# Feed-forward networks that begin by tiles of tokens, and GpSimd without elementwise work at stage boundaries

## The chip, the cores and the metric

The kernel runs on one core of one Trainium2 chip. The metric is the device time of one execution in microseconds (us). The engines are TensorE (PE; its weight loads are listed as PEld), VectorE (DVE), ScalarE (ACT), GpSimd (POOL), and SyncE (SP), whose queue issues the transfers.

## What is computed

256 tokens of 1024 columns pass two blocks. The first has two layers (attention, mixture of experts, an embedding gate). The second, which the change is mostly about, is:

```python
n = modulate(rmsnorm(h, g_ffn1[l]), sh1, sc1)
h = h + 0.5 * gt1 * swiglu(n, w1_gate[l], w1_up[l], w1_down[l])
n = modulate(rmsnorm(h, g_mix[l]), sh2, sc2)
h = h + gt2 * hybrid_mixer(n, w_in[l], w_pool[l], pool_scale[l], w_out[l])
n = modulate(rmsnorm(h, g_ffn2[l]), sh3, sc3)
h = h + 0.5 * gt3 * swiglu(n, w2_gate[l], w2_up[l], w2_down[l])
return rmsnorm(h, g_final)
```

`swiglu(n, wg, wu, wd)` is `(silu(n @ wg) * (n @ wu)) @ wd` with 2816 hidden columns, and `modulate(n, shift, scale)` is `n * (1 + scale) + shift`. The shifts, scales and gates are nine vectors from `silu(c) @ w_ada + b_ada`.

## The kernel before

All of h [128 partitions, 2 tiles of tokens, 1024] stays in SBUF. Products are in three passes over fp32r parts: an operand is split into a high part `hi` and what it leaves, `lo`, and `mm3` (L302 to 306) issues hi·hi, hi·lo and lo·hi. Weights come in units of 1 MB (`unit`, nine buffers `raw`) and are split in halves of a unit by `halves` (L278): ACT writes `hi` (L291), and DVE writes `lo` as raw minus hi (L292). There are four buffers of each, so four halves at most. While the counter `self.aside` is not zero, `lo` is made by POOL instead of DVE: for the first four halves behind each modulation, and for one piece at the start of each embedding gate.

`modulated_T` begins each of the three stages of the second block (FFN 1, mixer, FFN 2). It computes 1/rms of both tiles of tokens (`rstd`: two ACT squares with a sum per tile, L334, then a chain of nine DVE operations on one column, L314 to L337), fills PE with the columns of w_ada that are planned there (`fill`, `ada`, L1447), transposes h on PE, lays 1/rms along the rows (`rbc`), and then makes for each of the 8 blocks of columns f = h·gain·rbc (DVE), hi = f + shift (ACT), lo = f + shift − hi (DVE). For the mixer it does this by tiles of tokens (`head`, L403 to 411); for the two FFNs over all 256 tokens at once (L419 to 427).

An FFN goes over groups of 4 (last 2) blocks of 128 hidden columns. `dense_T` has the weight stationary and the 256 tokens moving, so gate and up come out transposed; a tanh on ACT and two DVE operations make the hidden values, which are split again (`hT`) and go into `down` one group later. `dense` has the tokens stationary and 512 weight columns moving; with `tail` (or `head`) its last (or first) chunk takes all of the first tile of tokens, then all of the second, and keeps all four split halves until the second pass. `add_gated` adds the last product of a stage to h (L1482, L1483), `finish` norms the rows and writes them out.

The order of the instructions on each engine is made by the framework's scheduler from the program order, the readiness by its own model, and a priority: `ahead_by(name)` moves instructions that many places ahead (`K["hp"]`: rstd 30, silu 200, split 60). Each engine then executes its queue in that order.

Of the kernel before, what the change touches and what calls it, by code (L numbers as in the profile page):

```python
# [8 lines left out]
F32 = mybir.dt.float32  # L9
F32R = mybir.dt.float32r  # L10
# [6 lines left out]
P = 128  # L17
# [41 lines left out]
class Packed:  # L59
    """Columns of a [128, n] array by name."""  # L60
# [55 lines left out]
def moving_units(w, widths, step=4):  # L116
    """Blocks of 128 rows by `step`, one after the other, a column chunk at a time."""
# [79 lines left out]
class Block:  # L197
    def __init__(self, ctx, tc, A, out, c_at, m_at, s_at, dbg=None):
# [14 lines left out]
        self.flip = 0  # L213
        self.waiting = []
# [3 lines left out]
    # -- small helpers -------------------------------------------------  # L218
# [59 lines left out]
    def halves(self, raw, n, k):  # L278
        """The unit's two parts, in halves of k/2 blocks of rows: f32r high parts and what they leave."""
# [28 lines left out]
    def rsqrt(self, y, v, n):  # L308
        """y = 1/sqrt(v/n) for positive v and n = 4**j: Newton's steps from the exponent's guess."""
# [14 lines left out]

    def rstd(self, tiles=(0, 1)):
        """1/rms of each token's row of h, a column for each of the tiles of tokens."""
        nc = self.nc
        n = len(tiles)
        with self.ahead_by("rstd"):
            ss = self.stat([P, n, 2], "ss")  # L330
            for half in range(2):
                for i, t in enumerate(tiles):
                    junk = self.wk.tile([P, 512], BF16, tag="xn", name="junk", bufs=4)
                    nc.scalar.activation(junk, self.h[:, t, half * 512:(half + 1) * 512], AF.Square,  # L334
                                         accum_out=ss[:, i, half:half + 1])
# [15 lines left out]
    def gained_T(self, gains, head):  # L351
        """h by each of the gains, transposed and in two parts; 1/rms is left to the products' rows."""
# [34 lines left out]
    def modulated_T(self, gain, shift, fill, head=False):  # L387
        """The normed rows by gain plus shift, transposed and in two parts."""
        nc = self.nc
        r = [self.rstd([t]) for t in range(2)]  # L390
        self.fill(*fill)
        self.aside = K["aside"]
        self.fine = bool(K["fmod"])
        with self.ahead_by("mod"):
            hi, lo = self.e([P, KT, T], F32R), self.e([P, KT, T], F32R)
            if head:
                for t in range(2):
                    sl = slice(t * P, (t + 1) * P)
                    ps = [self.psb([P, 4, P]) for _ in range(2)]
# [12 lines left out]
                return hi, lo  # L412
            ps = [self.psb([P, 2, T]) for _ in range(KT // 2)]
            pr = self.psa([P, T])
            rb = self.wk.tile([P, T], F32, tag="xn", name="rbc", bufs=4)
            for t in range(2):
                sl = slice(t * P, (t + 1) * P)
                for kk in range(KT):
                    nc.tensor.transpose(ps[kk // 2][:, kk % 2, sl], self.h[:, t, kk * P:(kk + 1) * P], self.ident)  # L419
                nc.tensor.transpose(pr[:, sl], r[t].to_broadcast([P, P]), self.ident)  # L420
                nc.vector.tensor_copy(rb[:, sl], pr[:, sl])
            for kk in range(KT):
                f = self.wk.tile([P, T], F32, tag="xn", name="xn", bufs=4)
                g, b = gain[:, kk:kk + 1], shift[:, kk:kk + 1]
                nc.vector.scalar_tensor_tensor(f, ps[kk // 2][:, kk % 2], g, rb, op0=OP.mult, op1=OP.mult)
# [1241 lines left out]
```

## Time and profile before

| | us |
|---|---|
| times of three runs | 1141.69, 1140.62, 1138.66 |
| median | 1140.62 |
| span of the profiled execution | 1135.9 |
| median less that span | 4.7 |
| PE busy, DVE busy, ACT busy, POOL busy | 1070.6, 701.9, 516.2, 74.3 |

The span goes from the first to the last instruction of the profiled execution; which of the times is that execution's is not listed, so the 4.7 us is taken from the median. A busy PE here means that matmuls are in flight: a matmul's listed duration is longer than the distance to the next one's start, so products are costed by the distance of starts.

### The profile page before, as it was taken

What the parts mean: (1) busy time and instruction counts of PE and PEld (TensorE: products, weight loads), DVE (VectorE), ACT (ScalarE), POOL (GpSimd) and SP (SyncE); (2) the same over time, 40 slices, a digit from 0 to 9 for tenths busy, and PEclk for the clock granted to TensorE, in tenths of its full rate; (3) what the DMA queues carried; (4) which work ended last, traced back from release to release, by engine and by line L of the source; (5) the groups of instructions that cost most, each with busy time, mean ns of one, the idle gap of its engine ahead of it and who ended that gap; (6) DMA issues with size and microseconds to landing.
All of it is one profiled execution on the core that took longest, in us unless ns stands there. A gap on an engine that the chain in (4) does not pass through costs nothing.

```text
span 1135.9 us, 18442 instructions
## 1 busy us (share of the span) xinstructions
PE 1070.6 (94%) x7133; PEld 833.2 (73%) x7133; DVE 701.9 (62%) x1672; ACT 516.2 (45%) x995; POOL 74.3 (7%) x61
## 2 busy tenths in 40 slices
PE   7999999999989999998987999999989979999995
PEld 6885548666457667665545999899879759999994
DVE  6786784644378966543467656565684775554555
ACT  5446584222267674221254444433544634444443
POOL 3000000210010002100003000000210030000001
PEclk9999999899999999999999999999989989999998
DMA  9746767599975485798886456745675344554401
GB/s 375 296 185 262 277 225 304 196 372 396 416 273 170 180 336 198 286 389 323 314 350 242 168 186 213 284 173 186 224 301 175 123 185 149 174 187 159 146 22 38
DMA packets 46508, 268.57 MB, mean 236 GB/s; under 512 B 5328, under 2 KB 7120, under 8 KB 20432
## 3 DMA queue, kind: packets, MB, share of 16 engines
q1 hardware_dynamic: 46416, 267.34, 62.9%
q8 instruction: 58, 0.95, 0.3%
q14 instruction: 34, 0.28, 0.1%
HBM read 266.27 MB, written 1.05 MB: 235 GB/s over the span
## 4 chain that ended last, share of the span: by engine, by line
PE 46%; DVE 5%; ACT 1%; issue 0%; ACTq 0%; DVEq 0%
PE b L305 8%; PE b L304 8%; PE b L306 8%; PE a L304 5%; PE a L306 5%; PE a L305 5%; PE a L1054 1%; DVE nq L319 1%; DVE h L1483 1%; PE a L1094 1%; DVE rstd L323 1%; PE a L1107 1%; PE b L1460 1%; DVE w L1482 1%; PE b L1033 0%
## 5 line engine op out<-in xcount | busy, mean ns | idle before, releaser
L292 DVE TENSOR_TENSOR lo<-raw,hi 128x1024 fp32r<-128x1024 f32 (+2 forms) x220 | 256.1, 1167 | 197.7 <-ACT hi L291 195.5
L291 ACT ACTIVATE hi<-raw 128x1024 fp32r<-128x1024 f32 (+2 forms) x234 | 234.3, 1008 | 262.3 <-PE b L305 144.6
L304 PE MATMUL b<-e,hi 128*128 128x256 f32 x768 | 219.7, 286 | 2.9 <-ACT e L426 2.9
L305 PE MATMUL b<-e,hi 128*128 128x256 f32 x768 | 219.3, 285 | 0.1
L306 PE MATMUL b<-e,lo 128*128 128x256 f32 x768 | 218.9, 285 | 0.0
L304 PE MATMUL a<-hi,e 128*128 128x512 f32 (+2 forms) x512 | 199.9, 391 | 2.4 <-ACT e L364 1.8
L305 PE MATMUL a<-lo,e 128*128 128x512 f32 (+2 forms) x512 | 198.0, 387 | 0.0
L306 PE MATMUL a<-hi,e 128*128 128x512 f32 (+2 forms) x512 | 197.2, 387 | 0.5 <-DVE e L365 0.5
L304 PEld LDWEIGHTS b<-e,hi 128*128 128x128 f32 x768 | 149.2, 194 | 4.7 <-ACT e L426 3.6
L305 PEld LDWEIGHTS b<-e,hi 128*128 128x128 f32 x768 | 149.1, 194 | 1.0 <-DVE e L427 0.7
L306 PEld LDWEIGHTS b<-e,lo 128*128 128x128 f32 x768 | 149.1, 194 | 0.0
L304 PEld LDWEIGHTS a<-hi,e 128*128 128x128 f32 x512 | 96.8, 189 | 23.1 <-ACT e L364 2.9
L306 PEld LDWEIGHTS a<-hi,e 128*128 128x128 f32 x512 | 96.1, 188 | 20.7 <-DVE e L365 2.1
L305 PEld LDWEIGHTS a<-lo,e 128*128 128x128 f32 x512 | 96.9, 189 | 18.9 <-DVE lo L292 0.9
L1054 PE MATMUL a<-raw,e 128*32 128x256 f32 x832 | 73.5, 383 | 1.1 <-DVEq L1291 0.8
L579 ACT ACTIVATE p<-p,m 128x128 f32<-128x128 f32 (+1 forms) x96 | 42.6, 447 | 8.9 <-DVE m L574 6.6
L484 DVE TENSOR_TENSOR h<-h,a 128x512 f32<-128x512 f32 x48 | 32.0, 684 | 22.0 <-PE a L1107 14.7
L1054 PEld LDWEIGHTS a<-raw,e 128*32 128x32 f32 x832 | 31.4, 109 | 18.8 <-issue 2.1
L292 POOL TENSOR_TENSOR lo<-raw,hi 128x1024 fp32r<-128x1024 f32 (+1 forms) x14 | 31.4, 2267 | 205.1 <-ACT hi L291 205.0
L1097 ACT ACTIVATE w<-a,sv 128x512 fp32r<-128x512 f32 x32 | 21.6, 687 | 48.0 <-PE a L1094 47.6
L1094 PE MATMUL a<-wd,hT 128*32 128x512 f32 x256 | 43.3, 607 | 0.0
L1107 PE MATMUL a<-w,GT 128*128 128x512 f32 x128 | 36.3, 416 | 6.2 <-ACT w L1097 5.1
(322 smaller groups left out, 1424.3 us busy)
## 6 DMA issues: line engine op xcount, KB each, us to landing
raw<-in_ffn SPq DMA_DIRECT2D x62, 1024.0 KB, 4.8
raw<-in_moe_gu SPq DMA_DIRECT2D x52, 1024.0 KB, 8.4
raw<-in_w_ada SPq DMA_DIRECT2D x36, 1024.0 KB, 5.0
wd<-in_moe_dn SPq DMA_DIRECT2D x64, 512.0 KB, 7.0
raw<-in_w_gate SPq DMA_DIRECT2D x8, 1024.0 KB, 11.1
raw<-in_w_m_in SPq DMA_DIRECT2D x8, 1024.0 KB, 5.5
raw<-in_w_a_in SPq DMA_DIRECT2D x7, 1024.0 KB, 11.1
e<-in_moe_gu SPq DMA_DIRECT2D x6, 1024.0 KB, 9.5
```

The source lines that it names most:

```text
L291: nc.scalar.activation(hi[:, sl], raw[:, at], AF.Copy)
L292: eng.tensor_tensor(lo[:, sl], raw[:, at], hi[:, sl], op=OP.subtract)
L304: mm(out, l[0], r[0], start=start, stop=False, **kw)
L305: mm(out, l[0], r[1], start=False, stop=False, **kw)
L306: mm(out, l[1], r[0], start=False, stop=stop, **kw)
L319: nc.vector.scalar_tensor_tensor(q, y, h, y, op0=OP.mult, op1=OP.mult)
L484: self.nc.vector.tensor_tensor(self.h[:, t, sl], self.h[:, t, sl], ps, op=OP.add)
L579: nc.scalar.activation(p, p, AF.Exp, bias=m[:, i:i + 1], scale=-1.0, accum_out=den[:, i:i + 1])
L1054: nc.tensor.matmul(pgs[pp][32 * x:32 * x + 32], xg[:, k, o:o + 32], wg[kk][:, x], start=(k == 0), stop=(k == KT - 1))
L1094: nc.tensor.matmul(py[32 * x:32 * x + 32], hT[:, 32 * x:32 * x + 32], wd[2 * n + x // 2][:, x % 2], start=True, stop=True)
L1097: nc.scalar.activation(yh[:, sl], py, AF.Identity, scale=cw)
L1107: nc.tensor.matmul(ps, GT[:, t * P:(t + 1) * P], y[:, n * 512:(n + 1) * 512], start=(b == 0), stop=(b == len(back) - 1))
```

## The change

- `self.aside` goes: every `lo` of a weight is made by DVE.
- `modulated_T` always goes by tiles of tokens: 1/rms, transposes and modulation of the first tile, then 1/rms of the second, the fill with w_ada columns, and the second tile.
- The sums of squares are issued where the last addition to h is made (`square_new`, in the second embedding gate and in `add_gated`), a half row at a time, and `rstd` takes them from there.
- The first group of each FFN uses `dense` with `head` for gate and up (tokens stationary), the hidden values are made in rows, and PE transposes them; the other groups stay.
- The PSUM banks of `down` (`acc`) are taken only after the first group. The w_ada products of the fills at stage starts use the pool `pa`, and their copies to SBUF come after the modulation (`later`).
- `finish` multiplies by 1/rms and by the gain in one DVE operation; before, POOL multiplied by the gain, and ACT and DVE by 1/rms.
- Docstrings and comments go (no instruction depends on them).

```diff
-                eng = nc.vector if self.aside == 0 or j < pieces - 1 else nc.gpsimd
...
+    def square(self, out, t, half):
+        junk = self.wk.tile([P, 512], BF16, tag="xn", name="junk", bufs=4)
+        self.nc.scalar.activation(junk, self.h[:, t, half * 512:(half + 1) * 512], AF.Square, accum_out=out)
+
+    def square_new(self, ci, t):
+        if ci + t == 0:
+            self.squares = self.stat([P, 2, 2], "squares", bufs=1)
+        with self.ahead_by("rstd"):
+            self.square(self.squares[:, t, ci:ci + 1], t, ci)
...
-    def modulated_T(self, gain, shift, fill, head=False):
-        r = [self.rstd([t]) for t in range(2)]
-        self.fill(*fill)
-        self.aside = K["aside"]
+    def modulated_T(self, gain, shift, fill, head=True):
+        hi, lo = self.e([P, KT, T], F32R), self.e([P, KT, T], F32R)
+        r = [None, None]
         with self.ahead_by("mod"):
             if head:
                 for t in range(2):
                     sl = slice(t * P, (t + 1) * P)
+                    r[t] = self.rstd([t])
+                    if t:
+                        self.squares = None
+                        self.fill(*fill)
...
+        for rows, ps in self.copies:
+            self.copy(rows, ps)
...
             self.nc.vector.tensor_tensor(self.h[:, t, sl], self.h[:, t, sl], y, op=OP.add)
+            self.square_new(ci, t)
...
-        acc = [[self.psa([P, 512]) for _ in range(2)] for _ in range(2)]
...
+            if gi == 0:
+                def put_up(ci, t, ps):
+                    with self.ahead_by("silu"):
+                        f = self.w4([P, 512])
+                        nc.scalar.activation(f, gates[t], AF.Tanh, scale=0.5)
+                        nc.vector.scalar_tensor_tensor(f, f, 1.0, gates[t], op0=OP.add, op1=OP.mult)
+                        nc.vector.scalar_tensor_tensor(f, f, 0.5, ps, op0=OP.mult, op1=OP.mult)
+                        rows.append(f)
+
+                off = self.dense(x, name, [512], lambda ci, t, ps: gates.append(ps), off, head=True)
+                off = self.dense(x, name, [512], put_up, off, head=True)
+                nb = 0
+                for b in range(2):
+                    with self.ahead_by("silu"):
+                        ps = self.psb([P, 2, T])
+                        for j in range(2):
+                            for t in range(2):
+                                nc.tensor.transpose(ps[:, j, t * P:(t + 1) * P],
+                                                    rows[t][:, (2 * b + j) * P:(2 * b + j + 1) * P], self.ident)
+                        self.parts(hT[0][:, 2 * b:2 * b + 2], hT[1][:, 2 * b:2 * b + 2], ps)
+            else:
+                for _ in range(2):
+                    off = self.dense_T(x, name, n, lambda b, ps: banks.append(ps), off)
...
-                nc.gpsimd.tensor_tensor(o[:, t, sl], self.h[:, t, sl], self.g_final[:, sl], op=OP.mult)
-            for half in range(2):
-                sl = slice(half * 512, half * 512 + 512)
-                self.copy(o[:, t, sl], o[:, t, sl], r)
+                nc.vector.scalar_tensor_tensor(o[:, t, sl], self.h[:, t, sl], r, self.g_final[:, sl], op0=OP.mult,
+                                               op1=OP.mult)
```

## Rows read from the trace of the kernel before

**Rows 1.** The page's busy time by engine (share of the span, count of instructions), and the granted clock of TensorE in 40 slices of the span, in tenths of full speed.

```profile
PE 1070.6 (94%) x7133; PEld 833.2 (73%) x7133; DVE 701.9 (62%) x1672; ACT 516.2 (45%) x995; POOL 74.3 (7%) x61
...
PEclk9999999899999999999999999999989989999998
```

**Rows 2.** Busy time of each engine in six stretches: from the last matmul of the stage before to the end of the first product of FFN 1, of the mixer and of FFN 2, each followed by the part of it in which the clock was low. Columns: stretch, its length, busy us and count of PE, PEld, DVE, ACT, POOL, granted clock, share of the DMA engines, GB/s.

```profile
609.80:638.40 28.60, 20.70 (x147) 17.01 (x147) 21.34 (x34) 12.87 (x20) 9.58 (x4) 0.82 0.64 246
619.70:629.90 10.20, 6.34 (x26) 5.76 (x27) 8.13 (x20) 2.75 (x7) 1.58 (x1) 0.50 0.88 371
821.00:844.10 23.10, 19.72 (x99) 13.91 (x99) 20.83 (x59) 12.71 (x29) 5.14 (x2) 0.85 0.79 314
827.90:834.70 6.80, 5.56 (x17) 4.33 (x18) 6.46 (x28) 2.04 (x7) 0.00 (x0) 0.50 1.01 426
920.00:947.10 27.10, 19.13 (x131) 16.21 (x131) 20.87 (x41) 9.78 (x17) 6.76 (x3) 0.81 0.47 180
926.90:937.10 10.20, 6.25 (x25) 5.16 (x26) 7.95 (x27) 3.82 (x9) 0.00 (x0) 0.50 0.67 281
```

**Rows 3.** Timeline of PE at the start of FFN 1: start, duration, engine, line, operation, operands, count of merged instructions, and in brackets the idle time before and what ended it.

```profile
611.62 1.90 PE L1447 MATMUL b<-raw,c 128*32 128x512 f32 x16
613.45 1.23 PE L419 MATMUL b<-consts,h 128*128 128x128 f32 x8
...
622.06 0.48 PE L420 MATMUL a<-consts,rstd 128*128 128x128 f32 x1 [6.41 <-DVE rstd L323]
623.98 0.58 PE L304 MATMUL b<-e,hi 128*128 128x256 f32 x1 [1.44 <-ACT e L426]
```

**Rows 4.** Timeline of DVE at the start of FFN 1: the first and last of the chain of tile 0, then a copy from PSUM, and from 613.21 the chain of tile 1.

```profile
607.47 0.16 DVE L337 SCALAR_TENSOR_TENSOR ssv<-ss 128x1 f32<-128x1 f32 x1 [0.79 <-ACT junk L334]
...
609.07 0.16 DVE L323 SCALAR_TENSOR_TENSOR rstd<-nq,rstd 128x1 f32<-128x1 f32 x1
...
612.04 0.69 DVE L267 COPY w<-b 128x512 f32<-128x512 f32 x1
613.21 1.17 DVE L337 SCALAR_TENSOR_TENSOR ssv<-ss 128x1 f32<-128x1 f32 x1 [0.48 <-ACT junk L334]
...
616.73 2.26 DVE L323 SCALAR_TENSOR_TENSOR rstd<-nq,rstd 128x1 f32<-128x1 f32 x1
...
622.90 1.27 DVE L425 SCALAR_TENSOR_TENSOR xn<-b,mods,rbc 128x256 f32<-128x256 f32 x3
...
625.27 1.26 DVE L425 SCALAR_TENSOR_TENSOR xn<-b,mods,rbc 128x256 f32<-128x256 f32 x3
```

**Rows 5.** Timeline of POOL at the same place.

```profile
611.69 9.58 POOL L292 TENSOR_TENSOR lo<-raw,hi 128x1024 fp32r<-128x1024 f32 x4 [23.60 <-ACT hi L291]
```

**Rows 6.** Timeline of DVE at the start of FFN 2.

```profile
917.93 1.92 DVE L337 SCALAR_TENSOR_TENSOR ssv<-ss 128x1 f32<-128x1 f32 x1 [1.70 <-ACT junk L334]
...
927.34 0.68 DVE L1482 TENSOR_TENSOR w<-a,w 128x512 f32<-128x512 f32 x1
```

**Rows 7.** Timeline of DVE at the start of the mixer; the last three are the modulation by tiles of tokens, three blocks of columns to a row.

```profile
822.55 2.68 DVE L1483 TENSOR_TENSOR h<-h,w 128x512 f32<-128x512 f32 x1
825.15 2.30 DVE L319 SCALAR_TENSOR_TENSOR nq<-rstd,nh 128x1 f32<-128x1 f32 x1
...
830.91 0.87 DVE L409 SCALAR_TENSOR_TENSOR xn<-b,mods,rbc 128x128 f32<-128x128 f32 x3
831.73 0.94 DVE L411 SCALAR_TENSOR_TENSOR e<-xn,mods,e 128x128 fp32r<-128x128 f32 x3
832.58 0.86 DVE L409 SCALAR_TENSOR_TENSOR xn<-b,mods,rbc 128x128 f32<-128x128 f32 x3
```

**Rows 8.** Timeline of PE around the mixer's first two products: the ends of a product with 512 columns moving, sixteen small matmuls between, and a product with 256 columns moving.

```profile
843.69 0.39 PE L305 MATMUL a<-lo,e 128*128 128x512 f32 x1
843.92 0.39 PE L306 MATMUL a<-hi,e 128*128 128x512 f32 x1
844.14 1.84 PE L1460 MATMUL b<-consts,w 128*128 128x1 f32 x16
845.85 0.37 PE L304 MATMUL b<-e,hi 128*128 128x256 f32 x1
...
846.53 0.28 PE L306 MATMUL b<-e,lo 128*128 128x256 f32 x1
846.65 0.28 PE L304 MATMUL b<-e,hi 128*128 128x256 f32 x1
```

**Rows 9.** Groups of instructions by line and shape in the stretch 600 to 835 us: busy us, mean ns of one, idle time before.

```profile
L292 DVE TENSOR_TENSOR lo<-raw,hi 128x1024 fp32r<-128x1024 f32 x59 | 72.2, 1224 | 63.3 <-ACT hi L291 61.4 <-DMA raw<-in_ffn 1.8
L291 ACT ACTIVATE hi<-raw 128x1024 fp32r<-128x1024 f32 x67 | 70.7, 1058 | 93.8 <-PE b L305 63.8 <-PE a L306 20.5 <-issue 7.9
...
L1524 DVE SCALAR_TENSOR_TENSOR w<-w,b 128x512 f32<-128x512 f32 x11 | 7.5, 681 | 0.0
...
L1523 ACT ACTIVATE w<-b 128x512 f32<-128x512 f32 x11 | 6.5, 589 | 2.4 <-PE b L306 2.4
```

**Rows 10.** Timeline of DVE at the end of the program.

```profile
1122.35 1.40 DVE L1483 TENSOR_TENSOR h<-h,w 128x512 f32<-128x512 f32 x1
...
1126.37 1.18 DVE L1483 TENSOR_TENSOR h<-h,w 128x512 f32<-128x512 f32 x1
...
1131.72 0.49 DVE L263 TENSOR_SCALAR e<-e,rstd 128x512 f32<-128x512 f32 x1
```

More of the change, by code (lines that the diff above doesn't have):

```diff
@@ L213, in __init__ @@
         self.flip = 0
+        self.squares = None
+        self.copies = []
         self.waiting = []
@@ L329, in rstd @@
         with self.ahead_by("rstd"):
-            ss = self.stat([P, n, 2], "ss")
-            for half in range(2):
[L332 to L335, printed above, removed]
+            if self.squares is not None:
+                ss = self.squares[:, tiles[0]:tiles[0] + n]
+            else:
+                ss = self.stat([P, n, 2], "ss")
+                for half in range(2):
+                    for i, t in enumerate(tiles):
+                        self.square(ss[:, i, half:half + 1], t, half)
             v = self.stat([P, n], "ssv")
@@ L411, in modulated_T @@
                         nc.vector.scalar_tensor_tensor(lo[:, kk, sl], f, b, hi[:, kk, sl], op0=OP.add, op1=OP.subtract)
[L412 to L425, printed above, removed]
-                nc.scalar.activation(hi[:, kk], f, AF.Identity, bias=b)
-                nc.vector.scalar_tensor_tensor(lo[:, kk], f, b, hi[:, kk], op0=OP.add, op1=OP.subtract)
+        for rows, ps in self.copies:
+            self.copy(rows, ps)
+        self.copies = []
         return hi, lo
@@ L1424, in ada_start, with ada @@
         self.mods = self.cp.tile([P, 9, KT], F32, name="mods")
-    def ada(self, n, psum):
+    def ada(self, n, psum, later=False):
         nc = self.nc
@@ L1449, in ada @@
         rows = self.w4([P, 512])
-        self.copy(rows, ps)
+        if later:
+            self.copies.append((rows, ps))
+        else:
+            self.copy(rows, ps)
         self.waiting.append((n, rows))
@@ L1483, in put @@
             self.nc.vector.tensor_tensor(self.h[:, t, sl], self.h[:, t, sl], y, op=OP.add)
+            self.square_new(ci, t)
         return put
@@ L1513, in ffn @@
             hT = (both[:, 0], both[:, 1])
-            banks = []
-            for _ in range(2):
-                off = self.dense_T(x, name, n, lambda b, ps: banks.append(ps), off)
+            banks, gates, rows = [], [], []
+            nb = n // 2
+            if gi == 0:
[17 more added lines that the diff above has]
+                        self.parts(hT[0][:, 2 * b:2 * b + 2], hT[1][:, 2 * b:2 * b + 2], ps)
+            else:
+                for _ in range(2):
+                    off = self.dense_T(x, name, n, lambda b, ps: banks.append(ps), off)
             self.ada_put()
-            nb = n // 2
             for b in range(nb):
@@ L1527, in ffn @@
             if pending:
+                if acc is None:
+                    acc = [[self.psa([P, 512]) for _ in range(2)] for _ in range(2)]
                 down(*pending)
@@ L1597, in finish @@
                 sl = slice(half * 512, half * 512 + 512)
-                nc.gpsimd.tensor_tensor(o[:, t, sl], self.h[:, t, sl], self.g_final[:, sl], op=OP.mult)
-            for half in range(2):
-                sl = slice(half * 512, half * 512 + 512)
-                self.copy(o[:, t, sl], o[:, t, sl], r)
+                nc.vector.scalar_tensor_tensor(o[:, t, sl], self.h[:, t, sl], r, self.g_final[:, sl], op0=OP.mult,
+                                               op1=OP.mult)
                 nc.sync.dma_start(self.out[t * P:(t + 1) * P, sl], o[:, t, sl])
@@ L1606, in fill @@
         for n in K["fill"].get(f"{where}:{j}", ()):
-            self.ada(n, self.psb if where.startswith("ffn") else self.psa)
+            self.ada(n, self.psb if where == "ffn0" else self.psa,
+                     where in ("ffn", "mixer"))
         if where in ("nsa", "moba"):
```

7 lines of the change are left out of this document (3 added, 4 removed).

## The prediction

> **What bounds the kernel now.** Read the page's busy times first [rows 1]: TensorE is busy 94% of the span, DVE 62%, GpSimd 7%. A share of 94% leaves little to win by feeding TensorE better in general, so the next view is where it does not run at full rate: the granted clock by slices shows single eights, and the windows show what lies there. At the start of FFN 1, mixer and FFN 2 the stretch from the last matmul of the stage before to the end of the first product is 28.6, 23.1 and 27.1 us long, and in each the clock falls to 0.50 (1.2 instead of 2.4 GHz) for 10.2, 6.8 and 10.2 us [rows 2].
>
> What must run on TensorE in them? Distances of starts at full clock are 0.23 us for 512 moving columns and 0.12 us for 256 [rows 8]. The mixer's first product is 48 of the first (11.0 us), an FFN's 96 of the second (11.5 us). Sixteen matmuls of w_ada take 1.9 us, eight transposes 1.2 us [rows 3]. FFN 1 fills with 32 of w_ada (two times 512 columns), the mixer with 32, FFN 2 with 16. So 3.8 + 2.4 + 11.5 = 17.7 us of work stands in 28.6; 3.8 + 2.4 + 11.0 = 17.2 in 23.1; 1.9 + 2.4 + 11.5 = 15.8 in 27.1. Lost are 10.9, 5.9 and 11.3 us, together 28 us: that is the stock from which the change can take.
>
> Who causes it? At FFN 1 TensorE waits 6.4 us for 1/rms of the second tile [rows 3]. The DVE timeline beside it has the same chain twice: for tile 0 from 607.47 to 609.23, 1.8 us for nine operations; for tile 1 a single operation on one column takes 1.17 or 2.26 us, so that the chain that began at 613.21 lets TensorE go on at 622.06 only [rows 4]. GpSimd makes its four `lo` parts just then, 9.6 us without a break [rows 5]. The mixer has the same (an addition to h takes 2.68 us, a chain operation 2.30) [rows 7], and FFN 2 (1.92), where moreover the additions for the second tile stand behind the slow chain in DVE's queue until 927.34 [rows 6]. Where GpSimd is silent the same chain is short. So the bound of these stretches is DVE, held up by GpSimd.
>
> The trace also shows which operations are held: the copy from PSUM at 612.04, under GpSimd's first `lo`, takes its usual 0.69 us [rows 4, 5]. The Trainium skill (SBUF — State Buffer, "Who interferes with whom") says that a DVE instruction contends with a GpSimd read when two inputs come from SBUF, and not with one. That rule speaks against one half of the change: the first operation of each modulation reads one tile from PSUM, so by it GpSimd could go on making `lo` beside these for nothing, and moving them costs DVE 1.22 us each; by the rule alone the gain would shrink by that, by rows the sum below has it in.
>
> **The change part by part.**
>
> *GpSimd's `lo` go to DVE.* A half costs DVE 1.22 us [rows 9], four per stage 4.9 us. How many lie on the path differs. At FFN 2, DVE stood idle before 917.93 (1.7 us) and will be idle again between the short chain and the last addition at 920, so I put three of four there; at the mixer two were made before the last additions (POOL had 5.1 us of its busy time, two of the four, inside the stretch [rows 2]); at FFN 1 I count all four on the path.
>
> *By tiles of tokens.* Modulation of three blocks of 128 tokens takes DVE 1.67 us (830.91 to 832.58) [rows 7], so both tiles are 16 × 0.557 = 8.9 us; all 256 at once took 0.79 us a block (622.90 to 625.27) [rows 4], 6.3 us. That is 2.6 us more DVE per FFN. The Trainium skill (VectorE: DVE Perf Modes, "The TRN2 errata") warns of just this: many small tiles pay a fixed cost each; an estimate from its 58 cycles at 0.96 GHz would be 16 × 0.06 = 1.0 us, and the rows say more. In return the first tile's modulation runs while TensorE still has the fill and the second tile's transposes, and the product on tile 0 needs only tile 0.
>
> *The new ends.* FFN 1, from 609.8: the last addition to h, allowed 0.9 us of ACT first, then 1.4 us; chain of tile 1 1.8; two `rbc` 0.6; modulation 8.9; `lo` 4.9. DVE is through at 628.3, and the last three matmuls (0.7) end at 629.0. TensorE's own sum ends at 609.8 + 3.8 + 2.4 + 11.0 = 627.0. I take 629.5 against 638.4: 8.9 us. FFN 2, from 920.0: 1.4 + 1.8 + 0.6 + 8.9 + 1.2 puts DVE at 933.9, the end at 934.6; TensorE's sum is 1.9 + 2.4 + 11.0, at 935.3, and 1.2 us for the wait on the second tile's chain makes 936.5 against 947.1: 10.6 us. Mixer, from 821.0: rest of the additions 1.8, two chains 3.6, 0.6, 8.9 and 2.4 put DVE at 838.3, the end at 839.0; with 1.0 us of waiting 840.0 against 844.1: 4.1 us. Bounds: lower, with all `lo` ahead of the modulations in DVE's queue and part of the clock loss kept, 4, 7 and 1 us; upper, TensorE's own sums, 11.4, 11.8 and 5.9 us. I take values near the upper ends since the DVE sums, which are the later ones, are from rows of the same operations.
>
> *New waits and queues.* In TensorE's queue the transpose of tile 0's 1/rms now stands ahead of the fill and of tile 1's transposes, which wait with it; at the FFNs that chain is through when TensorE arrives (609.23 against 609.8 [rows 2, 4]), at the mixer it is not, hence the 1.0 us. The fill's transfers keep their place in SP's queue, behind the stage before and ahead of the FFN's weights; their buffers come free 1.2 us later, which nobody notices, as all four halves of the first weight were there by 621 [rows 5].
>
> *Squares.* Before, too, the first halves were squared as soon as they were final, and between the last addition and the chain lies under a microsecond (0.79 of waiting at 607.47 [rows 4]). I cost it at nothing, between 0 and 1 us of gain per stage; the cover is ACT's idle time, and without it a square would wait for one `hi`, 1.06 us [rows 9].
>
> *The first group's form.* For `up`, 48 × 0.23 = 11.0 instead of 11.5 us, twice 0.5 gained. Eight more transposes per FFN, 1.2 us each time, 2.4 lost. They wait for a tanh and two DVE operations, 0.59 + 2 × 0.68 = 2.0 us [rows 9]; if TensorE's queue has them right behind `up`, it stands that long, otherwise the next group's matmuls cover it: 0 to 2.0 us per FFN, I take 0.3. Sum −2.0, bounds −5.4 and −1.4. The late copies of w_ada wait on nothing that TensorE needs, since two of the four banks of `pa` (those of the `rbc` transposes) are free by then; a bank taken from the copies instead would cost one copy, 0.69 us.
>
> *The end.* GpSimd's multiplications stretch additions to h to 1.40 and 1.18 us [rows 10] instead of 0.69, three of them, about 1.8 us, and one chain operation by 1.0. Against that, four DVE operations of about 0.69 us stand where two of 0.49 ran beside ACT; the last one ends 0.9 us later for it. Net 2.0 us, bounds 0 and 3.5.
>
> *Sum:* 8.9 + 10.6 + 4.1 − 2.0 + 2.0 = 23.6 us. The profiled span 1135.9 becomes 1112.3; with the 4.7 us between span and median, 1117. The bounds give gains of 6.6 (4 + 7 + 1 − 5.4 + 0) to 31.2 us, 1134 to 1109.
>
> **The rivals.**
>
> *DVE becomes the bound of the stretches.* All four `lo` on the path in each stage, ahead of the modulations; TensorE still idles long enough for the low clock. For it: DVE is already busy 20.8 of 23.1 us in the mixer's stretch [rows 2], and this kind of order is the scheduler's choice, which no row shows. Against it: `split` goes only 60 places ahead, into the modulation. It gives the lower bounds, 1134.
>
> *Split tiles are refilled too late (slower).* With `head` all four halves are held until the second tile's pass frees them, one per 6 matmuls (1.4 us). A refill is `hi` 1.06 and then `lo` 1.22 us [rows 9]: pipelined it keeps pace, one after the other it takes 2.3. If DVE's and ACT's other work (modulation, tanh, `put_up`) makes refills serial, the first pass of the product behind each `head` product loses 4 × 0.9 = 3.6 us; there are four such in the two FFNs, 14.4 us. With the lower-bound gains of 6.6 that is 1140.6 + 7.8 = 1148, and from two such passes (7.2 us) on it is slower than before. Against it: the mixer's first product has this form now, its last matmuls still start 0.23 us apart, and the next product follows right behind 16 small matmuls of 1.84 us [rows 8].
>
> *It is not GpSimd.* If the long operations had another cause that stays (the w_ada units landing at the same time, say), only 2 us at the end and the losses remain: 1139 to 1142. Against it: the long ones end with GpSimd's `lo` (9.58 us from 611.69 to 621.27) [rows 5], and the same chain was short before.
>
> **How the numbers follow.** Forecast 0.72, DVE as bound 0.16, not GpSimd 0.05, late refills 0.07. The likeliest time is 1117. The range 1108 to 1133 reaches from just past the upper bounds into the first rival and leaves out some 0.2. A measurement of this kernel can tell 0.3% (3.4 us) from no change; faster by more 0.88, within 0.05, slower 0.07.
>
> **What would show it.** In the new trace: no `lo` on POOL; chain operations of 0.15 to 0.22 us throughout; the three stretches near 19.7, 19.0 and 16.5 us; the clock low for less than the 27 us of before; the first product of an FFN as 48 matmuls at 0.23 us. It is wrong if the chain is short and TensorE still waits on L409 to L411 or on L292 (first rival), if `hi` waits on PE in the first group and TensorE waits on it (second), or if the chain stays long (third).

## The result, and the profile after

The changed kernel takes 1119.72 us (median of 4 runs, 1118.80 to 1120.68) against 1140.42 us for the kernel before in the same rounds: a ratio of 0.9825, 95% interval 0.9807 to 0.9844. That is 20.7 us faster, inside the forecast's 1108 to 1133. The profiled execution took 1120.68 us with a span of 1118.9; span and time are 1.8 us apart, not the 4.7 of the forecast. Single executions scatter: the kernel before took 1136.20 to 1142.63 us in eleven of them, with mean granted clocks from 0.978 down to 0.972.

The busy times of the page and the clock by slices, to be read beside [rows 1]:

```profile
PE 1066.2 (95%) x6957; PEld 821.9 (73%) x6957; DVE 698.3 (62%) x1720; ACT 518.9 (46%) x1009; POOL 37.8 (3%) x43
...
PEclk9998999899999999999999999999999999999998
```

POOL has lost half of its work, and the two eights that stood for the starts of the mixer and of FFN 2 are gone (the low stretch of FFN 1 lay across two slices and showed no eight). The eights that are left stand before 610 us and at the end.

Next the windows of the changed kernel: from the end of the stage before to the start of the second group of FFN 1, to the end of the mixer's first product, to the second group of FFN 2; then the part of each in which the clock was low (columns as in [rows 2]).

```profile
608.50:644.00 35.50, 32.73 (x170) 24.10 (x169) 28.03 (x64) 20.13 (x34) 0.00 (x0) 0.95 0.66 249
813.40:835.10 21.70, 18.68 (x99) 12.21 (x98) 18.04 (x61) 12.46 (x27) 0.00 (x0) 0.92 0.75 305
911.10:943.70 32.60, 28.87 (x141) 21.40 (x140) 24.45 (x63) 16.63 (x30) 0.00 (x0) 0.95 0.53 194
618.40:621.80 3.40, 3.40 (x10) 2.63 (x9) 3.40 (x10) 1.15 (x4) 0.00 (x0) 0.50 1.00 419
819.80:823.20 3.40, 3.40 (x23) 0.85 (x16) 2.75 (x11) 2.26 (x7) 0.00 (x0) 0.50 0.98 412
915.30:918.70 3.40, 3.40 (x18) 0.76 (x18) 2.74 (x15) 1.30 (x4) 0.00 (x0) 0.51 0.87 308
```

The two FFN windows are longer than those of [rows 2], since gate and up are interleaved now and the gate's end is no longer a milestone. The same windows of the kernel before:

```profile
609.80:651.70 41.90, 34.00 (x260) 30.31 (x259) 28.48 (x42) 19.25 (x28) 9.58 (x4) 0.88 0.61 226
...
920.00:959.50 39.50, 31.53 (x236) 28.61 (x235) 27.81 (x48) 15.26 (x23) 6.76 (x3) 0.87 0.50 187
```

So the starts shrank by 6.4 us (FFN 1), 6.9 (FFN 2) and, with the 23.10 us of [rows 2], by 1.4 (mixer). The clock stood at 0.50 for 10.2 us in all three, against 27.2. Behind the starts little happens: from the second group on, FFN 1 takes 169.4 us (before 169.3), the mixer from its second product 76.0 (76.0), FFN 2 165.1 (164.4).

PE's timeline at the start of FFN 1, beside [rows 3]:

```profile
608.50 1.03 PE L418 MATMUL b<-consts,h 128*128 128x128 f32 x8
...
609.57 3.64 PE L1450 MATMUL a<-raw,c 128*32 128x512 f32 x32
613.14 1.09 PE L418 MATMUL b<-consts,h 128*128 128x128 f32 x8
616.99 0.29 PE L419 MATMUL a<-consts,rstd 128*128 128x128 f32 x1 [2.75 <-DVE rstd L325]
617.04 0.48 PE L306 MATMUL a<-hi,e 128*128 128x512 f32 x1
```

Of 6.41 us of waiting for the second tile's 1/rms, 2.75 are left, and the 1.44 between it and the first product are gone. DVE's timeline shows what the 2.75 us are:

```profile
612.09 1.22 DVE L294 TENSOR_TENSOR lo<-raw,hi 128x1024 fp32r<-128x1024 f32 x1
613.22 0.15 DVE L351 SCALAR_TENSOR_TENSOR ssv<-squares 128x1 f32<-128x1 f32 x1
...
615.16 1.22 DVE L294 TENSOR_TENSOR lo<-raw,hi 128x1024 fp32r<-128x1024 f32 x1
616.30 0.21 DVE L321 SCALAR_TENSOR_TENSOR nq<-rstd,nh 128x1 f32<-128x1 f32 x1
...
616.69 0.15 DVE L325 SCALAR_TENSOR_TENSOR rstd<-nq,rstd 128x1 f32<-128x1 f32 x1
```

Each operation of the chain is short again (0.14 to 0.21 us, against 1.17 and 2.26 in [rows 4]), but the chain from 613.22 to 616.84 takes 3.6 us instead of 1.8: one `lo` and six operations of the first tile's modulation stand in it, and another `lo` right ahead of it.

The mixer, where least was won; PE's timeline:

```profile
815.21 0.63 PE L418 MATMUL b<-consts,h 128*128 128x128 f32 x4 [0.37 <-DVE nq L321]
818.50 0.32 PE L419 MATMUL a<-consts,rstd 128*128 128x128 f32 x1 [2.65 <-DVE rstd L325]
818.75 5.34 PE L1450 MATMUL a<-raw,c 128*32 128x512 f32 x32
...
824.09 0.47 PE L306 MATMUL a<-hi,e 128*128 128x512 f32 x1
```

PE waits 2.65 us for the first tile's 1/rms, and only then does the fill come, 5.34 us instead of 3.64, since the clock is low by now. In the kernel before the fill stood ahead of that wait. At FFN 2 PE waits as long, ahead of the second tile's last transposes:

```profile
915.26 0.39 PE L418 MATMUL b<-consts,h 128*128 128x128 f32 x1 [2.74 <-DVE rstd L325]
```

The end, DVE's timeline, beside [rows 10]:

```profile
1109.99 0.69 DVE L1489 TENSOR_TENSOR h<-h,w 128x512 f32<-128x512 f32 x1
```

The additions take 0.69 us and not 1.18 to 1.40. From the start of the last matmul (1108.76) to the end of the span it is 10.15 us, before 12.05.

### The profile page after: what moved, and what is told of

Read it like the earlier page. It is cut to its first block, busy times and chain, and to the rows that moved or that the text cites. A ratio compares the mean times of both kernels' runs of the same rounds, so it can differ in the third digit from the quotient of the medians.

```text
span 1118.9 us, 18106 instructions
## 1 busy us (share of the span) xinstructions
PE 1066.2 (95%) x6957; PEld 821.9 (73%) x6957; DVE 698.3 (62%) x1720; ACT 518.9 (46%) x1009; POOL 37.8 (3%) x43
## 3 DMA queue, kind: packets, MB, share of 16 engines
HBM read 266.27 MB, written 1.05 MB: 239 GB/s over the span
## 4 chain that ended last, share of the span: by engine, by line
PE 47%; DVE 3%; ACT 1%; issue 1%; DVEq 0%; ACTq 0%
PE b L306 7%; PE b L307 7%; PE b L308 7%; PE a L306 6%; PE a L308 6%; PE a L307 6%; PE a L1056 1%; DVE lo L294 1%; PE a L1096 1%; PE a L1450 1%; PE a L1109 1%; PE b L1466 1%; DVE w L1488 1%; DVE h L1489 0%; PE b L1035 0%
## 5 line engine op out<-in xcount | busy, mean ns | idle before, releaser
L294 DVE TENSOR_TENSOR lo<-raw,hi 128x1024 fp32r<-128x1024 f32 (+2 forms) x234 | 271.5, 1164 | 187.6 <-ACT hi L293 186.7
L306 PE MATMUL a<-hi,e 128*128 128x512 f32 (+2 forms) x576 | 225.3, 392 | 1.8 <-ACT e L378 1.8
L307 PE MATMUL a<-lo,e 128*128 128x512 f32 (+2 forms) x576 | 223.7, 389 | 0.0
L308 PE MATMUL a<-hi,e 128*128 128x512 f32 (+2 forms) x576 | 222.8, 389 | 0.0
L306 PE MATMUL b<-e,hi 128*128 128x256 f32 x640 | 181.8, 284 | 0.0
L307 PE MATMUL b<-e,hi 128*128 128x256 f32 x640 | 181.4, 283 | 0.0
L308 PE MATMUL b<-e,lo 128*128 128x256 f32 x640 | 181.3, 283 | 0.0
L306 PEld LDWEIGHTS a<-hi,e 128*128 128x128 f32 x576 | 109.1, 190 | 25.0 <-ACT e L378 2.9
L308 PEld LDWEIGHTS a<-hi,e 128*128 128x128 f32 x576 | 108.8, 189 | 22.9 <-DVE e L379 1.1
L307 PEld LDWEIGHTS a<-lo,e 128*128 128x128 f32 x576 | 109.2, 190 | 21.5 <-DVE lo L294 1.2
L306 PEld LDWEIGHTS b<-e,hi 128*128 128x128 f32 x640 | 123.0, 192 | 1.1 <-ACT hi L293 0.8
L307 PEld LDWEIGHTS b<-e,hi 128*128 128x128 f32 x640 | 123.0, 192 | 0.3
L308 PEld LDWEIGHTS b<-e,lo 128*128 128x128 f32 x640 | 122.9, 192 | 0.0
L1035 PE MATMUL b<-G,e 128*128 128x256 f32 x256 | 38.9, 298 | 3.3 <-DVE ssv L351 2.0
## 6 DMA issues: line engine op xcount, KB each, us to landing
raw<-in_w_a_in SPq DMA_DIRECT2D x7, 1024.0 KB, 10.9
```

Of the source, the lines that this page charges most:

```text
L294: eng.tensor_tensor(lo[:, sl], raw[:, at], hi[:, sl], op=OP.subtract)
L306: mm(out, l[0], r[0], start=start, stop=False, **kw)
L307: mm(out, l[0], r[1], start=False, stop=False, **kw)
L308: mm(out, l[1], r[0], start=False, stop=stop, **kw)
L1035: nc.tensor.matmul(ps[:, j], xh[part][:, t, sl], G[:, t], start=(t + j + part == 0), stop=(t + part == 2), skip_group_check=True)
```

## The experiments

The theory behind the forecast: GpSimd's subtractions hold up DVE's small operations at the stage starts, and taking them away is what counts. The rival after the result: tiles of tokens, early squares and the first group's form bring a good part of it themselves. The table gives for each kernel the median, and from PE's timeline of its profiled execution the lengths of the stages (from 0.23 us after the start of the last matmul of the stage before) and of the tail from the start of the last matmul, where FFN 2 ends too, to the span's end. "GpSimd idle" means that it makes no `lo`; the multiplications at the end stay with it unless the end is new. The stages ahead of FFN 1 are almost untouched by all these kernels, yet their end falls anywhere between 606.6 and 610.8 us; lengths of stages are therefore the better comparison.

| kernel | median us | up to FFN 1 | FFN 1 | mixer | FFN 2 | tail |
|---|---|---|---|---|---|---|
| before | 1140.42 | 609.8 | 211.2 | 99.1 | 203.8 | 12.1 |
| changed | 1119.72 | 608.5 | 204.9 | 97.7 | 197.7 | 10.2 |
| before, GpSimd idle | 1123.30 | 609.2 | 207.7 | 94.3 | 198.2 | 12.1 |
| before, GpSimd idle, new end | 1119.35 | 606.6 | 207.7 | 94.2 | 198.2 | 10.1 |
| changed, GpSimd busy | 1130.64 | 609.4 | 208.6 | 101.0 | 201.6 | 10.2 |
| changed, first group old | 1130.07 | 610.8 | 208.0 | 97.6 | 202.1 | 10.2 |
| changed, squares old | 1132.97 | 608.3 | 208.4 | 101.9 | 202.0 | 10.2 |
| changed, squares old, chains first | 1119.56 | 608.3 | 204.9 | 97.7 | 196.9 | 10.1 |
| changed, chains first | 1120.29 | 608.5 | 204.9 | 97.7 | 197.7 | 10.1 |
| changed, fill first | 1116.72 | 607.7 | 204.8 | 94.1 | 197.8 | 10.2 |
| changed, `lo` behind the chain | 1120.52 | 609.2 | 206.5 | 97.4 | 196.0 | 10.3 |
| changed, fill first, `lo` behind | 1120.21 | 608.9 | 205.3 | 97.9 | 197.0 | 10.3 |
| changed, fill first, `lo` in pieces | 1113.16 | 608.5 | 204.2 | 93.6 | 195.1 | 10.3 |
| before, GpSimd idle, new end, pieces | 1119.20 | 608.8 | 206.6 | 93.7 | 198.3 | 10.3 |

**GpSimd alone, in the kernel before.**

```diff
-    aside=4,
+    aside=0,
...
-    aside_ple=1,
+    aside_ple=0,
```

> The kernel before, with one edit: the counter that sends weight low parts to GpSimd stays zero, so DVE makes them all; everything else is as before. Theory (GpSimd's reads hold DVE's short chain): chain operations of 0.15 to 0.22 us at all three stage starts, but four low parts of 1.22 us more on DVE; roughly half of the change's 20.7 us, 1126 to 1132 us. Rival (the order by tiles of tokens brings the gain, GpSimd is incidental): 1137 to 1141 us.

1123.30 us, ratio 0.9865 (0.9847 to 0.9883), 2.7 us below the theory's range: a larger gain than it expected. Two numbers in a table of settings bring 16 of the 20.7 us. From DVE's and then PE's timeline at FFN 1:

```profile
616.08 1.21 DVE L292 TENSOR_TENSOR lo<-raw,hi 128x1024 fp32r<-128x1024 f32 x1
617.21 0.21 DVE L319 SCALAR_TENSOR_TENSOR nq<-rstd,nh 128x1 f32<-128x1 f32 x1
```

```profile
618.12 0.32 PE L420 MATMUL a<-consts,rstd 128*128 128x128 f32 x1 [3.02 <-DVE rstd L323]
```

Four `lo` more stand in DVE's queue at this start now, and still PE waits only 3.02 us for the second tile's 1/rms in place of 6.41. The edit does two things, it frees DVE and it shortens a `lo` from some 2.4 us to 1.21; but none of PE's waits from 609 us on in the kernel before ended with a `lo`, and 13.8 us of them ended with 1/rms.

**The reverse: the changed kernel, with the first four `lo` behind each modulation back on GpSimd.**

```diff
         self.copies = []
+        self.aside = 4
         return hi, lo
```

> The changed kernel, with GpSimd making the low parts of the first four weight halves behind each modulation again; tiles of tokens, squares and the end of the program stay as changed. Theory (GpSimd holds the chain): chain operations above 1 us again and 1127 to 1135 us. Rival (tiles of tokens brings the gain; DVE is the bound, so relieving it of 4.9 us per stage helps): 1112 to 1120 us.

The line in `halves` that chooses the engine by `self.aside` still stands in the changed kernel, where the counter is never set; so one line is enough. 1130.64 us, ratio 0.9927 (0.9908 to 0.9946): 10.9 us given back, as the theory said. Timelines of DVE and then of POOL at its FFN 1:

```profile
614.15 0.14 DVE L316 TENSOR_SCALAR nh<-ssv 128x1 f32<-128x1 f32 x1
...
614.53 1.75 DVE L321 SCALAR_TENSOR_TENSOR nq<-rstd,nh 128x1 f32<-128x1 f32 x1
616.20 0.34 DVE L424 SCALAR_TENSOR_TENSOR xn<-b,mods,rbc 128x128 f32<-128x128 f32 x1
616.46 2.12 DVE L325 SCALAR_TENSOR_TENSOR rstd<-nq,rstd 128x1 f32<-128x1 f32 x1
618.62 2.26 DVE L321 SCALAR_TENSOR_TENSOR nq<-rstd,nh 128x1 f32<-128x1 f32 x1
```

```profile
611.27 9.59 POOL L294 TENSOR_TENSOR lo<-raw,hi 128x1024 fp32r<-128x1024 f32 x4 [67.82 <-ACT hi L293]
```

Under the same four subtractions of POOL, the chain's operations on one column with two inputs from SBUF take 1.75 to 2.26 us. The chain's `nh`, with one input from SBUF, takes its usual 0.14 among them, and so does the modulation's first operation, on 128 columns of which the tile comes from PSUM, with 0.34. PE waits 6.84 us for the second chain and the clock falls, as in the kernel before.

**The first group as before, on the changed kernel.**

```diff
-            if gi == 0:
+            if False:
```

> The changed kernel, with the first group of each FFN in the old form (weights stationary, 256 tokens moving, no transposes of hidden values); modulation stays by tiles of tokens. Theory: the old form needs both tiles' modulation for its first blocks, so TensorE starts 3 to 5 us later per FFN, less the 1 us that the transposes cost: 1123 to 1128 us. Rival (the form itself only costs, as TensorE waits for the second tile's chain anyway): 1116 to 1119 us.

1130.07 us, ratio 0.9924 (0.9905 to 0.9942); slower than both expectations. PE's timeline:

```profile
619.30 0.29 PE L419 MATMUL a<-consts,rstd 128*128 128x128 f32 x1 [2.75 <-DVE rstd L325]
623.41 0.79 PE L306 MATMUL b<-e,hi 128*128 128x256 f32 x2 [3.82 <-ACT e L425]
```

With 256 tokens moving, the first matmul needs both tiles and so the second tile's modulation: 4.1 us behind the transposed 1/rms instead of 0.05. In the two FFNs the old form costs 3.2 and 4.4 us. Another 2.3 of the 10.3 us lie ahead of FFN 1, where nothing differs; this execution shows 3.4 us of low clock from 530.7 us on, where the changed kernel's shows none.

**The squares as before, on the changed kernel.**

```diff
     def square_new(self, ci, t):
+        return
```

> The changed kernel, with the sums of squares issued in rstd again, not where the additions to h are made. Theory: the scheduler issues them as soon as they are ready in either place: 1118.5 to 1121 us, no difference beyond 0.1%. Rival (the early squares shorten the chain's start): 1122 to 1125 us.

1132.97 us, ratio 0.9957 (0.9940 to 0.9974): 13 us lost, far outside both expectations. The first row is from PE's timeline, the second from ACT's:

```profile
621.30 0.45 PE L420 MATMUL a<-consts,rstd 128*128 128x128 f32 x1 [7.29 <-DVE rstd L325]
```

```profile
616.12 0.63 ACT L329 ACTIVATE junk<-h 128x512 bf16<-128x512 f32 x1 [1.38 <-DVE e L427]
```

The second tile's squares start at 616.12, when h has been final since 610.7: they stand in ACT's queue behind the first tile's modulation, and ACT waits for an operation of that modulation. Their scratch shares its four buffers with the modulation's tiles. Two things could be priced here, the place of the squares in the queue or the early squares as such. The next experiment tells them apart.

**The squares as before, but both chains written ahead of the loop over tiles.**

```diff
-        r = [None, None]
+        r = [self.rstd([t]) for t in range(2)]
...
-                    r[t] = self.rstd([t])
```

> The changed kernel with the squares back inside rstd, and both tiles' rstd written ahead of the loop over tiles, as the kernel before has them. Theory (in the fourth experiment the squares themselves were cheap; what cost 13 us is that the second tile's squares stood behind the first tile's modulation on ACT and for the scratch buffers): 1120 to 1125 us. Rival (squares taken after the stage's end cost that much wherever they stand): 1130 to 1134 us.

1119.56 us, ratio 0.9820 (0.9794 to 0.9846), level with the changed kernel. Squaring early is worth nothing; what cost 13 us was that the second tile's squares were written behind the first tile's modulation. Whether the shared scratch or the place in the queue does it wasn't tried apart.

**Chains first, early squares kept.** The same edit without the `return`.

> The changed kernel, early squares kept, with both tiles' rstd written ahead of the loop over tiles. Theory (the second tile's transposed rstd stands ahead of the first product in TensorE's queue and waits for a chain that is put together only among the first tile's modulation and the lo subtractions): the second rbc transpose comes about 3 us sooner in FFN 1 and the mixer, 1112 to 1117 us. Rival (DVE's total work up to the first product is the same in either order, so the first product waits for the same sum): 1117.5 to 1122 us.

1120.29 us, ratio 0.9831 (0.9806 to 0.9857). The theory falls, the rival holds: PE's three starts come within 0.2 us of the changed kernel's. DVE's order at the starts of the two FFNs is the same to the operation, at the mixer a few operations change places. That the chain goes ahead by its priority anyway is the likely reason; it wasn't tried.

**GpSimd idle and the new end, nothing else.** The first experiment's edit and, in `finish`, the one DVE operation:

```diff
-                nc.gpsimd.tensor_tensor(o[:, t, sl], self.h[:, t, sl], self.g_final[:, sl], op=OP.mult)
-            for half in range(2):
-                sl = slice(half * 512, half * 512 + 512)
-                self.copy(o[:, t, sl], o[:, t, sl], r)
+                nc.vector.scalar_tensor_tensor(o[:, t, sl], self.h[:, t, sl], r, self.g_final[:, sl], op0=OP.mult,
+                                               op1=OP.mult)
```

> The kernel before with GpSimd idle at the three stage boundaries and with the end's one DVE operation for each half, but without tiles of tokens, early squares or the first group's new form. Theory (these three bring nothing net up to the last product; the end brings 1.9 us on its own): 1120 to 1122.5 us, that is the first experiment's 1123.3 less 1.9, and not more than 2.5 us from the changed kernel. Rival (the end's gain needs the early squares, which free ACT and DVE there, or tiles of tokens bring several us that the first experiment's lower spread hid): 1123 to 1126 us. The tail from the last matmul to the span's end should be near 10.1 us by the theory, 12 by the rival.

1119.35 us, ratio 0.9830 (0.9807 to 0.9853), tail 10.1 us. This small edit reaches the changed kernel's time. The large part of the change (tiles of tokens, early squares, new first group) is worth nothing net, as far as the scatter of the medians tells: by the table it gains 2.8 us in FFN 1 and 0.5 in FFN 2, and loses 3.4 in the mixer.

**The fill ahead of the first 1/rms, at the mixer and FFN 2.**

```diff
         r = [None, None]
+        early = fill != ("ffn", 0)
+        if early:
+            self.fill(*fill)
...
-                        self.fill(*fill)
+                        if not early:
+                            self.fill(*fill)
```

> The changed kernel with the fill of modulation products (the ada matmuls) issued ahead of the first tile's rstd at the mixer and at FFN 2, as the kernel before had it, instead of behind the first tile's transposed rstd. Theory (at the mixer 5.2 us of fill stand in TensorE's queue between the first and the second rbc transpose, after 2.65 us of idleness; at FFN 2 3.3 us after 2.74): the fill moves into the idleness, the mixer's first product comes near 821 instead of 824.1 and FFN 2's near 2 us sooner, 1113 to 1117 us. Rival (the second tile's rstd and modulation on DVE set the start, the fill only fills): the first products come within 1 us of the changed kernel's, 1118.5 to 1121 us.

1116.72 us, ratio 0.9804 (0.9783 to 0.9825): 3.0 us, the theory's range. PE's timeline at the mixer:

```profile
812.60 3.64 PE L1454 MATMUL a<-raw,c 128*32 128x512 f32 x32
816.17 1.86 PE L422 MATMUL b<-consts,h 128*128 128x128 f32 x15
818.05 0.32 PE L423 MATMUL a<-consts,rstd 128*128 128x128 f32 x1
...
819.60 0.32 PE L423 MATMUL a<-consts,rstd 128*128 128x128 f32 x1 [1.12 <-DVE rstd L325]
```

The fill now lies under the chain, and the first product starts 7.2 us into the stage instead of 10.7. That is the mixer's 3.6 us. FFN 2 gains nothing (197.8): there PE waits 0.73 us ahead of the first tile's 1/rms and 3.27 for the second chain, in place of 2.74 and 0.99.

**DVE's first four `lo` of a stage behind the second chain.** Each of these subtractions is queued behind the chain's last operation (`self.behind` counts four halves down from the end of each `modulated_T`):

```diff
+                    with self.tc.issue_after(self.chain.ins) if self.behind else nullcontext():
-                    eng.tensor_tensor(lo[:, sl], raw[:, at], hi[:, sl], op=OP.subtract)
+                        eng.tensor_tensor(lo[:, sl], raw[:, at], hi[:, sl], op=OP.subtract)
```

> The changed kernel with DVE's subtractions for the first four halves of weights of each of the three stages queued behind the end of the second tile's rstd chain, so that none of them (1.22 us each) stands among its ten small operations. Theory (in the changed kernel TensorE idles 2.65 to 2.75 us at each of the three starts for a chain that has one to three such subtractions in it, 1.2 to 3.7 us): the second rbc transpose comes 1 to 2.5 us sooner in FFN 1 and FFN 2, while the first products may then stall for the parts: 1114 to 1119 us. Rival (the parts are needed as soon as the rows are, so the subtractions only change places with the chain): 1119 to 1124 us.

1120.52 us, ratio 0.9839 (0.9818 to 0.9860): the rival. PE's timeline at FFN 1:

```profile
615.41 0.29 PE L422 MATMUL a<-consts,rstd 128*128 128x128 f32 x1 [0.50 <-ACT hi L294]
615.47 0.48 PE L309 MATMUL a<-hi,e 128*128 128x512 f32 x1
619.18 0.79 PE L310 MATMUL a<-lo,e 128*128 128x512 f32 x1 [3.23 <-DVE lo L296]
```

The second 1/rms is laid along the rows 6.2 us into the stage instead of 8.5, and the wait comes back one matmul later, for `lo`. FFN 1 loses 1.6 us by it, while FFN 2 gains 1.7: there the first waits are 1.16 and 0.58 us and the clock stays at 1.00. With the fill first as well:

> The fill ahead of the first rstd at the mixer and FFN 2 (1116.7 us by itself) and the subtractions behind the second chain together. Theory (different waits, so the gains add): 1111 to 1116 us. Rival (with the fill first the subtractions come in time and their place no longer matters): 1116 to 1120 us.

1120.21 us, ratio 0.9836 (0.9812 to 0.9860), slower than both expectations; what the fill had brought is gone again. `lo` is needed as soon as the rows are, and where it is put behind the chain it stands ahead of the modulation: at the mixer two of them from 819.24, and PE waits 2.48 us for the first modulated block.

**The fill first, and these `lo` in four pieces of 256 columns.**

```diff
-                    eng.tensor_tensor(lo[:, sl], raw[:, at], hi[:, sl], op=OP.subtract)
+                    q = 4 if self.behind else 1
+                    for c in range(q):
+                        s0 = sl.start + c * o // q
+                        eng.tensor_tensor(lo[:, s0:s0 + o // q], raw[:, i * m + s0:i * m + s0 + o // q],
+                                          hi[:, s0:s0 + o // q], op=OP.subtract)
```

> The fill first as above, and the first four halves' subtractions on DVE cut into pieces of 256 columns, near a quarter of 1.22 us each with a small surcharge, so that the chain's operations can slip between them. Theory (what delays the chain is the grain of the subtraction, not its sum): 1112 to 1116.5 us. Rival (DVE's sum up to the first product decides; pieces add 0.1 us each): 1117 to 1121 us.

1113.16 us (1112.87 to 1116.28), ratio 0.9779 (0.9757 to 0.9801): the best of all, 26 us below the kernel before in the same rounds (1139.13). The groups by shape in 600 to 920 us, then PE's timeline at FFN 1 and at FFN 2, then the windows of the three starts:

```profile
L298 DVE TENSOR_TENSOR lo<-raw,hi 128x1024 fp32r<-128x1024 f32 x79 | 96.6, 1224 | 77.2 <-ACT hi L294 75.0 <-DMA raw<-in_ffn 1.9
L298 DVE TENSOR_TENSOR lo<-raw,hi 128x256 fp32r<-128x256 f32 x48 | 18.2, 420 | 3.8 <-ACT hi L294 3.8
```

```profile
615.22 0.30 PE L429 MATMUL a<-consts,rstd 128*128 128x128 f32 x1 [1.02 <-DVE rstd L331]
```

```profile
912.73 0.32 PE L429 MATMUL a<-consts,rstd 128*128 128x128 f32 x1 [2.39 <-DVE rstd L331]
```

```profile
608.50:643.00 34.50, 31.71 (x168) 22.38 (x167) 28.46 (x76) 20.24 (x34) 0.00 (x0) 1.00 0.66 253
812.70:831.00 18.30, 17.42 (x106) 12.59 (x105) 18.04 (x67) 12.70 (x28) 0.00 (x0) 1.00 0.92 367
906.30:937.00 30.70, 28.31 (x146) 21.70 (x146) 25.45 (x69) 17.38 (x30) 0.00 (x0) 1.00 0.57 209
```

A half costs DVE more (at 908.59 four quarters in a row take 1.43 us, against 1.22), yet inside the chains never more than one quarter stands between two operations, the waits shrink, and the clock is granted in full at all three starts.

**The pieces in the plain kernel** (GpSimd idle, new end, no tiles of tokens).

> The kernel before with GpSimd idle at the stage boundaries, the end's one DVE operation for each half, and the first four halves' subtractions on DVE in pieces of 256 columns; no tiles of tokens, no early squares, no new first group (without the pieces this measured 1119.35 us). Theory (the pieces free the chains of either order, but the whole-row order still has 1.8 to 2 us from the second rbc transpose to its first product, and in FFN 1 some 3 us that tiles of tokens save): 1115 to 1118.5 us, so the tiles are worth 2 to 5 us once fill and grain are right. Rival (the tiles bring nothing even then): 1111.5 to 1114.5 us, level with the fill-first kernel in pieces at 1113.2.

1119.20 us, ratio 0.9823 (0.9802 to 0.9843). It misses the theory's range by 0.7 us and the rival's by 4.7. By the median the pieces bring nothing here (1119.35 without them); by the table they shorten FFN 1 by 1.1 us and the mixer by 0.5, and this execution reaches FFN 1 some 2 us later, which hides it. The 6.0 us to the kernel above come from tiles of tokens together with the first group's form: 2.4 us in FFN 1 and 3.2 in FFN 2, while the mixers are equal (93.7 and 93.6). PE's waits here and in the kernel above, from 607 and 608 us on (us in total, times, longest), show the difference:

```profile
PE a L427 <- DVE rstd L329: 3.2, 2, 1.8
PE b L310 <- ACT e L433: 3.1, 2, 1.6
```

```profile
PE a L429 <- DVE rstd L331: 4.3, 3, 2.4
PE a L312 <- ACT e L435: 1.0, 1, 1.0
PE a L313 <- DVE lo L298: 0.8, 1, 0.8
```

With whole rows the first product of each FFN waits 1.65 and 1.45 us for the modulation behind the transposed 1/rms; in the kernel above FFN 2 has no such wait, and FFN 1 has the last two of its list, within the first group. And the clock stands at half for the first 6.8 and 3.4 us of the two products, where the kernel above has it in full:

```profile
617.80:624.60 6.80, 6.48 (x28) 6.19 (x29) 5.12 (x14) 3.07 (x7) 0.00 (x0) 0.50 1.01 426
918.20:921.60 3.40, 3.40 (x18) 3.40 (x18) 3.25 (x9) 1.31 (x3) 0.00 (x0) 0.50 1.01 426
```

## Why the prediction was right

**The cause was right.** GpSimd holds up DVE where two inputs lie in SBUF: taking it away brings 16 us in the kernel before, putting it back costs 11 in the changed one. The rival "it is not GpSimd" is out, and so is the late refill: of the first group's 96 matmuls in FFN 1 the last starts 24.3 us after the first, of which 21.9 are pitch (95 × 0.23) and 1.7 the low clock (3.4 us at half rate); in FFN 2 it is 22.0. The rows fit what the Trainium skill (SBUF — State Buffer, "Who interferes with whom") states: a DVE instruction with two inputs from SBUF contends with a GpSimd read, one with a single SBUF input doesn't. The trace agrees, with 1.75 us against 0.14 in one chain and 2.12 against 0.34 between two neighbours. By that rule GpSimd could have kept `lo` beside the first operation of each block alone; no kernel here does that.

**The terms.** The stages in the table give what each was worth. FFN 1: forecast 8.9 less 1.0 for the first group's form, 7.9; measured 6.3. FFN 2: 9.6; measured 6.1. Mixer: 4.1; measured 1.4. End: 2.0; measured 1.9. Another 1.3 us lie ahead of FFN 1, within the scatter of that point. So the span is 17.0 us shorter and not 23.6. That the median was still met to 2.7 us is luck: 4.7 us were added between span and time, and the changed kernel's profiled execution shows 1.8. Every execution listed with both has 1.7 to 1.9 between them, so some 2.9 of the 4.7 seem to be a profiled execution of the kernel before that ran faster than its median; its own time isn't listed.

**The step that was mis-sized** is DVE's order. The sums put the chain of the second tile at 1.8 us and `lo` at 1.22 each, one behind the other. The scheduler puts other work in between: at FFN 1 `lo` and the first tile's modulation into the second chain (3.6 us), at the mixer two `lo` into the first chain, at FFN 2 three `lo` (910.02, 911.23, 913.16) into the first chain and ahead of the second tile's additions. PE waits 2.65 to 2.75 us at each of the three starts, and 3.4 us of low clock follow. This is the first rival, "DVE becomes the bound", in part: with the 1.0 us booked for the first group's form, FFN 2 (7.1) and the mixer (1.4) gained no more than a little above its lower bounds of 7 and 1, FFN 1 (7.3) came nearer to the forecast. The forecast took values near its upper ends because the DVE sums were the later ones; at FFN 2 its own figures have DVE's end at 934.6, ahead of TensorE's 935.3. In pieces, the same work costs the chains less, and with the fill first that closes the gap: 1113.2 us, a span of 1111.7 against the forecast 1112.3.

**The mixer's 1.0 us** for the first tile's 1/rms ahead of the fill was the worst figure: the wait is 2.65 us, and the fill behind it runs at the low clock, 5.34 instead of 3.64. Moving the fill back brings 3.6.

**The squares** were costed at nothing, and that holds (1119.56 against 1119.72). But they must be ahead of the first tile's modulation in the program, one way or the other, or 13 us go.

**The first group's form** was booked as a cost of 2.0 us, with its use inside the stretches. The experiment gives its worth with modulation by tiles, 3.2 + 4.4 us. With the old form FFN 1 and FFN 2 take 208.0 and 202.1 us, against 207.7 and 198.2 in the kernel without tiles: without the form the tiles lose. That also answers what the forecast never asked: how much of the gain needs tiles of tokens at all. None: GpSimd idle and the new end reach the same time, and the tiles only pay, by 6 us, once the fill and the grain of `lo` are put right.

## What to carry to other kernels

When a small serial chain on one engine sets a stage's start, look first at which other engine's work stretches its operations, and then at what the scheduler can put between them; with the fill in its place, the grain of that work was worth 3.6 us here, though its sum grew. Test the small edit of a large change by itself: here two settings and one fused operation were worth all of it. A fill for an idle engine belongs ahead of the wait that it is to cover, in the queue of that engine.

## What the runs showed of the hardware

An idle stretch of PE of 2.65 to 2.75 us at each start was followed by 3.4 us at a granted clock of 0.50 (1.2 GHz); in the fill-first kernel in pieces, with waits of 1.02, 0.88 and 2.39 us there and two more of 0.80 and 0.97 in FFN 1's first group, the granted clock stayed 1.00 (2.4 GHz) at all three. So less waiting can gain up to 1.7 us a start beyond the wait itself, an estimate (half of 3.4). But the length of a wait doesn't settle it: every kernel here has a wait of 2.6 us that ends near 530 us, and the low clock followed in the profiled executions of two (before; changed with the first group old) and not in those of the other twelve.

The subtraction on 128 x 256 is listed with 420 ns and on 128 x 1024 with 1224 ns, that is 1.05 ns a column and some 150 ns fixed. The Trainium skill (VectorE: DVE Perf Modes, "The TRN2 errata") has (N + 151) cycles at 0.96 GHz for an fp32 `tensor_tensor`, by estimate 424 and 1224 ns: the rows agree. In a row the starts lie closer than the listed ends: four quarters take 1.43 us and not 1.68. For modulation by tiles the rows give distances of starts of 0.26 to 0.30 us on 128 columns and 0.40 on 256, so its 16 more operations cost 2 to 3 us, an estimate that bears out the forecast's 2.6 from rows. The forecast's estimate of 1.0 from the 58 cycles of that section was too low.
